# The gate products of a state-space branch, made in the linear-attention stage and kept in DRAM until the output stage

## The chip, the core and the metric

The kernel runs on one core of a Trainium2 chip. A core has five engines with instruction streams of their own: TensorE (PE, matrix products into PSUM), VectorE (DVE), ScalarE (ACT), GpSimd (POOL) and SyncE (SP), which here only starts transfers. The metric is the device time in microseconds; lower is better.

## The reference, cut to what matters

Two equal layers run one after the other over 2048 latent tokens and 128 context tokens. Each layer normalises `x` to `h`, projects `h` once, hands slices of the projection to three branches, and projects their joined outputs back:

```python
h = rms_norm(x, norm_w) * (1 + scale) + shift
z, xbc, dt, gq, gk, gv, gg, glr, aq, ak, av, ag = split_proj(h @ w_in)
y_ssd, _ = ssd_branch(z, xbc, dt, ...)       # state-space scan, both directions
y_gla, _ = gla_branch(gq, gk, gv, gg, glr, ...)   # linear attention
y_att = latent_attention(...) * silu(ag)     # windowed attention
x = x + gate * (concatenate([y_ssd, y_gla, y_att]) @ w_out)

# the end of ssd_branch:
y = y_f + flip(y_b) + xs * d_skip
y = rms_norm(y * silu(z), norm_w)
```

`z` (512 wide) depends on `h` alone, and is used only at the very end of the state-space branch.

## The kernel before

The 2176 tokens are 17 tiles of 128: the context tile (CT) and tiles 0 to 15. `h` is kept transposed for the whole layer as two fp16 parts (high and low), so `prod` (L281) makes a product of 256 columns as 24 matmuls of 128x256. A weight block of 256 columns is 1 MB; nine slots hold such blocks, and `ring` gives the next free one. `load_w` starts the transfer and splits the block into two fp16 parts on ACT and DVE (L246 to L265).

A layer has four stages.

1. The linear-attention (GLA) stage, `gla_phase`, goes through groups of tiles, CT alone first, then pairs. The generator `gla_group` makes the projections of a group (the first on the tile `HT`, the last a narrow one of 48 columns) and then, in the next group's turn, its chunk sums. Layer 0 takes the pairs upwards and makes `h` there, tile by tile; layer 1 takes them downwards, while the output stage of layer 0 has already made its `h`.
2. The attention stage, whose first matmuls after the GLA stage are `att_project`'s.
3. The state-space (SSD) stage: a convolution written as products, and a scan per tile.
4. The output stage, `out_tile`, in the order CT, 15, ..., 0. For each tile it fetches the branch outputs (`ym`), makes the gate product `z` (two products, 48 matmuls, L281, into `pz`), its Tanh (L1188) and gate (L1189), adds the backward scan's part (`pof`, L1197, L1200, L1201, with the carried state, L1203 and L1204), scales and squares (L1209, L1214), writes the normalised row in two fp16 parts to `yh` (L1231, L1232), has a DMA transpose it to `yt` (L1237), and makes four products with `w_out` (96 matmuls, into `po`), which L1247 and L1248 add to `x`. In layer 0 the same tile then makes the next layer's `h` (L429 to L466, another transpose). `yh` has one buffer, `yt` two.

The stages are written as Python generators that are stepped in turns; a scheduler then fixes the order of instructions on each engine at build time, so an engine works in that order and stops where its next instruction has to wait. All transfers are started by SP, in its order.

The two weight blocks of `z` (`wz0`, `wz1`) are loaded in the attention and SSD stages as loads 4 and 5 of `ssd_load`, and the four of `w_out` behind them; the last of those is converted on DVE (L264) while the scan is ending.

Of the kernel before, what the change touches and what calls it, by code (L numbers as in the profile page):

```python
# [10 lines left out]
F32 = mybir.dt.float32  # L11
# [9 lines left out]
P = 128  # L21
# [8 lines left out]
def host_constants(nt):  # L30
# [32 lines left out]
          ("sm", 512, 3), ("sxw", 512, 2), ("ssb", 512, 1), ("sy", 512, 2), ("sjd", 128, 1), ("scd", 8, 2)],  # L63
    "O": [("ym", 1024, 2), ("ct", 256, 2), ("sz1", 512, 1), ("oyo", 256, 1), ("sz0", 512, 1), ("yh", 1024, 1), ("yt", 1024, 2), ("xs", 1024, 2), ("gate", 1024, 1), ("otm", 512, 2),
          ("osb", 512, 1), ("hl", 1024, 1)],
# [3 lines left out]
START = {"A": 0, "T": 0, "C": 9600, "S": 0, "Q": 11136, "O": 0}  # L69
WORDS = 12768  # L70

# [7 lines left out]
def hybrid_kernel(ctx, tc, a, o):  # L79
# [146 lines left out]

    ring = [0, 1, 5, 7, 8, 2, 3, 6, 4]

# [76 lines left out]
    grow = [drp.tile([2, DM], F32, name=f"grow_{l}") for l in range(L)]  # L305
    mrow = [drp.tile([2, 2 * DM], F32, name=f"mrow_{l}") for l in range(L)]
    sct = [drp.tile([P, 2, P], F32, name=f"sct_{t}") for t in range(NTT)]
    sstb = [drp.tile([P, 512], F32, name=f"sstb_{t}") for t in range(NTT)]
# [166 lines left out]
    def gla_load(l, s, i):  # L475
        if i == 0:
            s.wqk, s.iqk = load_in(l, (1552, 1808), name="wqk")
        elif i == 1:
            s.wv, s.iv = load_in(l, (1808, 2064), name="wv")
        elif i == 2:  # L480
            s.wdl, s.idl = load_in(l, (1536, 1552), (2320, 2352), name="wdl", dst=k_wdl)

            s.aux = slot()
        else:
            s.wg, s.ig = load_in(l, (2064, 2320), name="wgg")

    def gla_begin(l, s, order):
# [502 lines left out]
    def ssd_load(l, s, i):  # L990

        if i < 4:
            w = load_in(l, (512 + 256 * i, 768 + 256 * i), name=f"wx{i}")
        elif i < 6:
            w = load_in(l, (256 * (i - 4), 256 * (i - 4) + 256), name=f"wz{i - 4}")
        else:
            w = load_w(a["w_out"], l, [(256 * (i - 6), 256 * (i - 6) + 256)], f"wo{i - 6}", row_scale=vec[l][:, 56:62])
        s.w.append(w)
# [157 lines left out]
    def out_begin(l, s):  # L1156
        s.wz, s.izh = [], []
        for j in range(2):
            w, iz = s.w[4 + j]
            izh = sb(f"izh{j}", [P, 1])  # L1160
            V.tensor_scalar(izh, iz, 0.5, None, ALU.mult)
            s.wz.append(w)
            s.izh.append(izh)
        s.wo, s.io = zip(*s.w[6:10])

        s.rows = halves(slot())
# [10 lines left out]
    def out_tile(l, s, t):  # L1177
# [89 lines left out]

    def gla_phase(l, s, order, before=None, after=None):

        prev, s.first = None, order[0]  # L1270
        for n, g in enumerate(order):
# [5 lines left out]
            run(prev)  # L1277
            step(cur)
            if after:
                after(n)  # L1280
            prev = cur
        run(prev)

    def loads(l, gla, att, ssd):

        todo = [(gla_load, gla, 0), (gla_load, gla, 1), (gla_load, gla, 2), (att_load, att, 0), (att_load, att, 1), (att_load, att, 2), (gla_load, gla, 3)]
        todo += [(ssd_load, ssd, i) for i in range(10)]

# [45 lines left out]
    def layer_state():  # L1334
        x = Gla(), Att(), Ssd()
        x[2].w = []
        return x
# [9 lines left out]

    gla_phase(0, gla, order0, enter, lambda n: load[0](3 + max(0, min(n - 3, 4))))
    for l in range(L):
        gla, att, ssd = state[l]  # L1350
        load[l](7)
        gla_states(l, gla)
        att_begin(l, att)
        load[l](8)
        gla_out_begin(l, gla)
# [15 lines left out]
        for t in range(NT):  # L1371
# [21 lines left out]
        for n, g in enumerate(order):  # L1393
# [8 lines left out]
            run(nxt)  # L1402
            load[l](13 + min(n, 3))
        load[l](17)
# [5 lines left out]
        for n in range(NTT):  # L1410
# [6 lines left out]
            run(tiles[n])  # L1417
            if l + 1 < L and n in (5, 8, 11):
                load[l + 1]((5, 8, 11).index(n) + 1)
        if l + 1 < L:  # L1420
            back = list(range(NG - 2, -1, -1))
            load[l + 1](3)
            gla_begin(l + 1, state[l + 1][0], back)
            gla_phase(l + 1, state[l + 1][0], [NG - 1] + back, None, lambda n: load[l + 1](3 + max(0, min(n, 4))))


def build(shapes, consts):
    import concourse.bacc as bacc

    nc = bacc.Bacc("TRN2", target_bir_lowering=False, num_devices=1, dynamic_dma_scratch_size=4096)  # L1430
    f32 = mybir.dt.from_np(np.dtype("float32"))
# [28 lines left out]
```

## Time and profile before

| what | us |
|---|---|
| median of 3 runs | 2339.43 (2337.83 to 2343.84) |
| the profiled execution: its own time | 2334.53 |
| the span that its trace covers | 2332.8 |
| TensorE busy in it | 2089.6 (90%) |
| VectorE, ScalarE, GpSimd busy | 1628.6, 991.8, 872.7 |

The profiled execution is 4.9 us below the median and 1.7 us above its own span. A share of busy time is a mean over stages that are limited by different things, so each stage is read by itself. In a row of the trace, "pd<-slot,HT" names the output and the operands by the program's names, and "[idle before <-releaser]" says how long the engine stood still before the row and what ended that.

### The profile page before, as it was taken

To read this page: it belongs to the slowest core of one execution; us is meant where nothing else is said; L and a number is where in the kernel's file an instruction comes from. 1 tells how busy PE (TensorE), PEld (TensorE's weight loads), DVE (VectorE), ACT (ScalarE), POOL (GpSimd) and SP (SyncE) were. 2 spreads that over 40 slices of the span, in tenths; PEclk is the share of its full clock that TensorE was granted. 3 is DMA by queue.
4 is the path that set the end of the run, shared out by engine and by line. 5 is a ranking of instruction groups with operands and counts; after the bars stand their busy time and mean duration, and the time that the engine had idled before them with its cause. 6 is when DMAs were issued, how large, how long until landed. Compare 5 with 4: busy or idle time off the path is not lost. (4 is left out here: it accounts for less than half of the span.)

```text
span 2332.8 us, 53735 instructions
## 1 busy us (share of the span) xinstructions
PE 2089.6 (90%) x21245; PEld 1735.9 (74%) x21245; DVE 1628.6 (70%) x4088; ACT 991.8 (43%) x2183; POOL 872.7 (37%) x906
## 2 busy tenths in 40 slices
PE   3688958899899999899999995888999999999998
PEld 0455747778787788788888884777878778878887
DVE  2566767887789888865564656777788988864442
ACT  2443545555445334433333643555563533422221
POOL 0010014566443444544431001456643344454442
PEclk6798979999999999999999997999999999999999
DMA  8697433567611013577656123456671101265643
GB/s 294 182 256 188 108 85 87 119 150 166 135 56 37 33 42 124 164 188 177 170 151 174 42 75 93 93 110 149 154 153 55 37 32 42 78 171 167 163 141 98
DMA packets 486353, 288.02 MB, mean 123 GB/s; under 512 B 354344, under 2 KB 447924, under 8 KB 483796
## 3 DMA queue, kind: packets, MB, share of 16 engines
q1 hardware_dynamic: 483796, 271.99, 44.5%
q0 software_dynamic: 2304, 12.58, 1.6%
q8 instruction: 167, 2.74, 0.5%
q14 instruction: 86, 0.70, 0.1%
HBM read 141.11 MB, written 64.93 MB: 88 GB/s over the span
## 5 line engine op out<-in xcount | busy, mean ns | idle before, releaser
L281 PEld LDWEIGHTS <-HT 128*128 128x128 f16 x6528 | 585.3, 100 | 170.8 <-issue 93.0
L281 PE MATMUL pd<-slot,HT 128*128 128x256 f16 x3456 | 432.1, 278 | 50.0 <-ACT work L806 29.7
L281 PEld LDWEIGHTS <-slot 128*128 128x128 f16 x4320 | 394.3, 97 | 105.9 <-issue 41.2
L281 PE MATMUL pd<-slot,work 128*128 128x256 f16 x3264 | 365.5, 273 | 2.1 <-DMA work<-work 2.1
L281 PEld LDWEIGHTS <-work 128*128 128x128 f16 x3264 | 319.2, 98 | 42.6 <-DMA work<-work 2.6
L281 PE MATMUL pd<-HT,slot 128*128 128x260 f16 (+3 forms) x2592 | 316.5, 269 | 13.2 <-DMA HT<-work 12.4
L281 PE MATMUL ps<-HT,slot 128*128 128x260 f16 (+1 forms) x1728 | 201.5, 270 | 4.5 <-DVE work L1054 4.5
L281 PE MATMUL ps<-slot,HT 128*128 128x256 f16 x1440 | 175.6, 281 | 19.1 <-ACT work L1188 14.3
L1248 POOL TENSOR_TENSOR work<-work 128x512 f32<-128x512 f32 x68 | 89.2, 1312 | 185.5 <-DVE work L1247 176.3
L875 POOL TENSOR_TENSOR work<-work 128x512 f16<-128x512 f32 (+2 forms) x102 | 117.4, 1154 | 85.1 <-ACT work L874 70.3
L1054 DVE SCALAR_TENSOR_TENSOR work<-ps,work 128x256 f32<-128x256 f32 (+1 forms) x288 | 134.0, 465 | 11.9 <-ACT work L1052 7.6
L1054 DVE SCALAR_TENSOR_TENSOR work<-pd,work 128x256 f32<-128x256 f32 (+1 forms) x288 | 132.5, 464 | 3.7 <-ACT work L1052 0.9
L872 ACT ACTIVATE work<-ps,nm,K 128x512 f32<-128x512 f32 (+2 forms) x136 | 100.9, 744 | 73.1 <-DVE nm L864 58.3
L1116 POOL TENSOR_TENSOR work<-work 128x512 f32<-128x512 f32 x68 | 73.2, 1081 | 113.3 <-ACT work L1074 61.8
L1056 ACT ACTIVATE work<-work 128x256 f32<-128x256 f32 (+1 forms) x144 | 58.1, 403 | 121.0 <-DVE work L1054 82.8
L1088 POOL TENSOR_TENSOR work<-K,work 128x512 bf16<-128x512 bf16 x68 | 72.2, 1063 | 77.9 <-PE ps L1100 77.2
L281 PE MATMUL pm<-slot,HT 128*128 128x256 f16 x816 | 98.8, 277 | 1.6 <-DVE work L907 1.5
L854 PEld LDWEIGHTS <-work 128*128 128x128 f16 x1008 | 74.4, 98 | 34.7 <-issue 31.9
L874 ACT CAST work<-work 128x512 f16<-128x512 f32 (+2 forms) x136 | 78.1, 589 | 46.2 <-DMA slot<-work 26.3
L669 POOL MEMSET work<- 128x512 f32 x2 | 1.1, 525 | 256.2 <-PE pm L616 256.2
L1057 DVE SCALAR_TENSOR_TENSOR work<-work 128x256 f32<-128x256 f32 (+1 forms) x144 | 81.9, 569 | 19.1 <-ACT work L1056 18.0
L1214 ACT ACTIVATE work<-work 128x512 bf16<-128x512 f32 x68 | 42.7, 629 | 119.2 <-DMA work<-work 53.6
(374 smaller groups left out, 4035.1 us busy)
## 6 DMA issues: line engine op xcount, KB each, us to landing
slot<-in_w_in_dram SPq DMA_DIRECT2D x24, 1024.0 KB
ymix<-work SPq DMA_DIRECT2D x68, 128.0 KB
yacc<-work SPq DMA_DIRECT2D x34, 256.0 KB
work<-ymix SPq DMA_DIRECT2D x34, 256.0 KB
work<-yacc SPq DMA_DIRECT2D x34, 256.0 KB
x<-work SPq DMA_DIRECT2D x17, 512.0 KB
work<-x SPq DMA_DIRECT2D x17, 512.0 KB
out_dram<-work SPq DMA_DIRECT2D x17, 512.0 KB
```

The lines of the kernel that those rows point to most:

```text
L281: T.matmul(out, lhsT=lhs(i, k), rhs=rhs(j, k), start=(n == 0), stop=(n == 3 * KB - 1))
L854: T.matmul(ps[:, bs], lhsT=s.qt[t][:, 2 * gg + kv], rhs=kt[:, 2 * kv + j], start=(j == 0), stop=(j == 1 and mk is None))
L872: S.activation(pr, sc[hh][:, :nb * P], AF.Exp, scale=s.isc[:, 0:1], bias=nm[:, hh:hh + 1], accum_out=ls[:, hh:hh + 1])
L874: S.copy(p16[:, 0], pr)
L875: (G if hh else V).tensor_tensor(p16[:, 1], pr, p16[:, 0], ALU.subtract)
L1054: V.scalar_tensor_tensor(acc[:, jj, :W], pp[:, q:q + W], s.cw[j][:, q, jj:jj + 1], acc[:, jj, :W], ALU.mult, ALU.add)
L1056: S.activation(th[:, :W], acc[:, jj, :W], AF.Tanh)
L1057: V.scalar_tensor_tensor(acc[:, jj, :W], th[:, :W], 1.0, acc[:, jj, :W], ALU.add, ALU.mult)
L1088: G.tensor_tensor(sr[:, j:j + 4], oh[:, j:j + 4].unsqueeze(2).to_broadcast([P, 4, P]), at.unsqueeze(1).to_broadcast([P, 4, P]), ALU.mult)
L1116: G.tensor_tensor(xw, x, bc8(s.wst[:, t, 8 * d:8 * d + 8]), ALU.mult)
L1214: S.activation(junk, ym[:, 512 * i:512 * i + 512], AF.Square, accum_out=ss[:, i:i + 1])
L1248: G.tensor_tensor(xs[:, js], xs[:, js], tm, ALU.add)
```

## The change

The gate products leave `out_tile`. A new `gate_tile` makes them in `gla_phase`: after each group's first step, for the tiles of the group before, and for the last group after its last step. It copies each half from PSUM to SBUF on ACT and stores it in DRAM (`zraw`). `out_tile` loads the tile's 512 columns back and takes the Tanh from there. The loads of the two weight blocks move to the GLA stage of the same layer (layer 0) or to the end of layer 0's output stage (layer 1), and the blocks of `w_out` come correspondingly earlier. The number of matmuls is the same. Per layer there are 34 more copies on ACT, 34 more stores (128 KB each) and 17 more loads (256 KB each).

```diff
-    ring = [0, 1, 5, 7, 8, 2, 3, 6, 4]
+    ring = [0, 1, 5, 7, 8, 2, 3, 4, 6]
...
+    def gate_load(l, s, i):
+        w, iz = load_in(l, (256 * i, 256 * i + 256), name=f"wz{i}")
...
+    def gate_tile(s, t):
+
+        pz = psum(None, "d")
+        for j in range(2):
+            js = slice(256 * j, 256 * j + 256)
+            prod(pz[:, js], hs(t), lambda q, k: s.wz[j][:, q, k, :])
+            z = k_hx[1][:, js]
+            S.copy(z, pz[:, js])
+            D.dma_start(zraw[t][:, js], z)
...
-        pz = psum(None, "d" if t in (CT, NT - 1) else "s")
-        sz = sb(rot(("sz0", "sz1"), "sz"), [P, 512])
+        z = sb("zl", [P, 512])
+        D.dma_start(z, zraw[t])
+        sz = sb("sz", [P, 512])
         for j in range(2):
             js = slice(256 * j, 256 * j + 256)
-            prod(pz[:, js], hs(t), lambda q, k: s.wz[j][:, q, k, :])
-            S.activation(sz[:, js], pz[:, js], AF.Tanh, scale=s.izh[j])
-        V.scalar_tensor_tensor(sz, sz, 1.0, pz, ALU.add, ALU.mult)
+            S.activation(sz[:, js], z[:, js], AF.Tanh, scale=s.izh[j])
+        V.scalar_tensor_tensor(sz, sz, 1.0, z, ALU.add, ALU.mult)
...
             run(prev)
             step(cur)
+            if n:
+                for t in GROUPS[order[n - 1]]:
+                    gate_tile(gates, t)
             if after:
                 after(n)
             prev = cur
         run(prev)
+        for t in GROUPS[order[-1]]:
+            gate_tile(gates, t)
...
-            for at, n in ((1, 9), (4, 10), (7, 11), (13, 12), (15, 13)):
+            for at, n in ((4, 11), (6, 12), (8, 13), (13, 14), (15, 15)):
```

Not shown: the order list of `loads` (the two gate blocks stand behind the third GLA block), the pool table (`zl` with two buffers in place of a second `sz`, the pool 768 words longer) and a smaller DMA scratch.

TensorE at the end of layer 0's GLA stage. Before, the last narrow projection (48 wide) is followed by the attention's two products (`slot7`, `slot8`), and between them stand the chunk sums of the last two groups (L589, L596):

```order
L281 MATMUL pd_3365<-K_77,HT_83 128x48
...
L281 MATMUL pd_3722<-slot7_74,HT_83 128x256
...
L281 MATMUL pd_3722<-slot8_75,HT_83 128x256
...
L281 MATMUL pd_3792<-slot7_74,HT_83 128x256
...
L281 MATMUL pd_3792<-slot8_75,HT_83 128x256
...
L589 MATMUL ps_3443<-work_66 64x64 x4
```

In the changed program the `z` products of four tiles (`pd_4171`, `pd_4224`, `pd_4433`, `pd_4486`; `slot7` and `slot8` now hold `wz0` and `wz1`) stand there, and the attention's (`pd_4688`, from `slot2`) follow. L607 is the old L589:

```order
L281 MATMUL pd_4171<-slot7_74,HT_83 128x256
...
L281 MATMUL pd_4224<-slot7_74,HT_83 128x256
...
L281 MATMUL pd_4433<-slot7_74,HT_83 128x256
...
L281 MATMUL pd_4433<-slot8_75,HT_83 128x256
...
L281 MATMUL pd_4486<-slot8_75,HT_83 128x256
...
L607 MATMUL ps_4303<-work_66 64x64 x4
...
L281 MATMUL pd_4688<-slot2_69,HT_83 128x256
```

So 192 matmuls of the gate stand ahead of the attention's 96, and all but three of them ahead of the last group's sums; in layer 1 it is the same.

VectorE in layer 0's output stage, where it writes the second fp16 part of a tile's row (L1232 before, L1241 after; `zc_13594` and `osc_13599` belong to one tile) and evicts a half of `po` (L1247, L1256; `osc` tells the tile). Before:

```order
L1247 SCALAR_TENSOR_TENSOR work_66<-pd_13478,osc_13171,work_66 128x512
L1216 TENSOR_SCALAR zss_13585<-zss_13585 128x1
...
L1224 TENSOR_TENSOR zc_13594<-zrs_13590,zc_13594 128x1
L1232 SCALAR_TENSOR_TENSOR work_66<-work_66,zc_13594 128x512 x2
L1247 SCALAR_TENSOR_TENSOR work_66<-pd_13529,osc_13171,work_66 128x512
L1228 TENSOR_SCALAR osc_13599<-zrb_13597 128x1
```

After, where `zc_14032` and `osc_14037` belong to one tile and `osc_13882` to the tile before it:

```order
L1233 TENSOR_TENSOR zc_14032<-zrs_14028,zc_14032 128x1
L1237 TENSOR_SCALAR osc_14037<-zrb_14035 128x1
L1241 SCALAR_TENSOR_TENSOR work_66<-work_66,zc_14032 128x512
L1256 SCALAR_TENSOR_TENSOR work_66<-pd_14071,osc_13882,work_66 128x512
L462 SCALAR_TENSOR_TENSOR work_66<-work_66,rs_14047,slot0_67 128x1024
L1241 SCALAR_TENSOR_TENSOR work_66<-work_66,zc_14032 128x512
```

Before, a tile's row was finished behind the eviction of the first half of the product two tiles ahead of it (between `osc_13171` and `osc_13599` lies one more tile, `osc_13396`). After, in 8 of the 15 pairs of neighbours in layer 0, the row is finished only behind the eviction of the first half of the very next tile's product; in the other pairs, and in layer 1, the distance is two, as before.

SP near the start of layer 0 (L350, L351 fetch `w_ada`; L466, L467 transpose `h`). Before:

```order
L350 DMA slot3_70<-in_w_ada_dram 128x1024 x2
L466 DMA_TRANSPOSE HT_83<-work_66 128x16x128
L1304 DMA slot5_72<-in_x_sample_dram 128x1024
L466 DMA_TRANSPOSE HT_83<-work_66 128x16x128
```

After:

```order
L467 DMA_TRANSPOSE HT_83<-work_66 128x16x128
L1318 DMA slot6_73<-in_x_sample_dram 128x1024
L467 DMA_TRANSPOSE HT_83<-work_66 128x16x128
L1318 DMA slot5_72<-in_x_sample_dram 128x1024
L619 DMA sqin_16_168<-work_66 32x2x128 x3
L351 DMA slot2_69<-in_w_ada_dram 128x1024
```

The four `w_ada` transfers of that place now stand behind the transposes of the first tiles.

## Rows read from the trace of the kernel before

**Rows 1.** The page: the span in 40 slices of 58.3 us, TensorE's busy tenths.
```profile
PE   3688958899899999899999995888999999999998
```

**Rows 2.** Windows: length, busy us (count) by engine, granted clock, DMA share, GB/s.
```profile
80.00:280.00 200.00, 161.09 (x2341) 118.59 (x2338) 126.02 (x308) 90.16 (x184) 16.69 (x29) 0.91 0.69 182
80.00:120.00 40.00, 26.38 (x298) 18.93 (x295) 22.75 (x47) 16.61 (x38) 4.63 (x8) 0.83 0.65 166
1280.00:1400.00 120.00, 119.66 (x2152) 100.63 (x2151) 76.09 (x238) 63.36 (x133) 0.00 (x0) 1.00 0.20 58
1000.00:1200.00 200.00, 190.33 (x1653) 167.03 (x1651) 120.09 (x243) 67.73 (x133) 92.42 (x92) 0.97 0.65 172
```

**Rows 3.** Timeline of TensorE, early layer 0: start, us, line, idle before.
```profile
93.53 4.43 PE L281 MATMUL pd<-HT,slot 128*128 128x256 f16 x25 [11.17 <-DMA HT<-work]
```

**Rows 4.** Timeline of TensorE, end of the GLA stage in layer 0, then layer 1.
```profile
282.90 2.23 PE L281 MATMUL pd<-slot,HT 128*128 128x256 f16 x19
...
301.99 0.54 PE L589 MATMUL ps<-work 32*64 32x64 f32 x32 [1.86 <-DVE work L578]
...
330.40 1.87 PE L281 MATMUL pd<-slot,HT 128*128 128x256 f16 x8 [15.34 <-ACT work L806]
...
1390.91 2.23 PE L281 MATMUL pd<-slot,HT 128*128 128x256 f16 x19
...
1409.49 0.54 PE L589 MATMUL ps<-work 32*64 32x64 f32 x32 [2.07 <-DVE work L578]
```

**Rows 5.** Timelines of SP and ACT, end of layer 1's GLA stage: a store and its waiter.
```profile
1397.06 6.07 SPq L599 DMA_DIRECT2D oacc<-work  x2
...
1402.41 0.37 ACT L598 COPY work<-pm 128x256 f32<-128x256 f32 x1 [4.99 <-DMA oacc<-work]
```

**Rows 6.** Timeline of TensorE, layer 0: last convolution product, `po` of tile 15, next layer.
```profile
922.15 2.86 PE L281 MATMUL ps<-HT,slot 128*128 128x260 f16 x24
...
987.99 10.64 PE L281 MATMUL pd<-slot,work 128*128 128x256 f16 x96
...
1249.38 2.84 PE L281 MATMUL pd<-HT,slot 128*128 128x128 f16 x48
```

**Rows 7.** Timeline of TensorE, layer 1, from the last convolution product to the end.
```profile
2024.82 2.86 PE L281 MATMUL ps<-HT,slot 128*128 128x260 f16 x24
...
2078.28 3.98 PE L281 MATMUL pd<-slot,work 128*128 128x256 f16 x35
...
2142.40 1.03 PE L1197 MATMUL ps<-K,work 128*128 128x256 f32 x4
2143.27 2.13 PE L281 MATMUL pd<-slot,work 128*128 128x256 f16 x18
2145.23 2.78 PE L281 MATMUL ps<-slot,HT 128*128 128x256 f16 x24
...
2299.75 27.02 PE L281 MATMUL pd<-slot,work 128*128 128x256 f16 x246
```

**Rows 8.** Timelines of SP and ACT, one tile of layer 1's output stage.
```profile
2156.56 1.91 SPq L1237 DMA_TRANSPOSE work<-work  x1
...
2160.62 0.63 ACT L1214 ACTIVATE work<-work 128x512 bf16<-128x512 f32 x1 [0.95 <-DMA work<-work]
...
2166.85 0.63 ACT L1214 ACTIVATE work<-work 128x512 bf16<-128x512 f32 x1 [1.73 <-DVE work L1209]
...
2173.15 1.83 SPq L1237 DMA_TRANSPOSE work<-work  x1
```

**Rows 9.** Timelines of SP, ACT, DVE, layer 0's output stage: transpose, landing, vector work.
```profile
1122.11 2.02 SPq L1237 DMA_TRANSPOSE work<-work  x1
...
1126.37 0.63 ACT L1214 ACTIVATE work<-work 128x512 bf16<-128x512 f32 x1 [1.06 <-DMA work<-work]
...
1129.53 1.22 DVE L462 TENSOR_TENSOR work<-work,slot 128x1024 f32<-128x1024 f32 x1
...
1137.03 0.75 DVE L1247 SCALAR_TENSOR_TENSOR work<-pd,osc,work 128x512 f32<-128x512 f32 x1
```

More of the change, by code (lines that the diff above doesn't have):

```diff
@@ L63 @@
           ("sm", 512, 3), ("sxw", 512, 2), ("ssb", 512, 1), ("sy", 512, 2), ("sjd", 128, 1), ("scd", 8, 2)],
-    "O": [("ym", 1024, 2), ("ct", 256, 2), ("sz1", 512, 1), ("oyo", 256, 1), ("sz0", 512, 1), ("yh", 1024, 1), ("yt", 1024, 2), ("xs", 1024, 2), ("gate", 1024, 1), ("otm", 512, 2),
+    "O": [("ym", 1024, 2), ("ct", 256, 2), ("zl", 512, 2), ("oyo", 256, 1), ("sz", 512, 1), ("yh", 1024, 1), ("yt", 1024, 2), ("xs", 1024, 2), ("gate", 1024, 1), ("otm", 512, 2),
           ("osb", 512, 1), ("hl", 1024, 1)],
@@ L69 @@
 START = {"A": 0, "T": 0, "C": 9600, "S": 0, "Q": 11136, "O": 0}
-WORDS = 12768
+WORDS = 13536
 ONCE = ("bm", "bn", "bx", "hcl", "hpb", "hrb", "hc", "hci")
@@ L306, in hybrid_kernel @@
     mrow = [drp.tile([2, 2 * DM], F32, name=f"mrow_{l}") for l in range(L)]
+    zraw = [drp.tile([P, 512], F32, name=f"zraw_{t}") for t in range(NTT)]
     sct = [drp.tile([P, 2, P], F32, name=f"sct_{t}") for t in range(NTT)]
@@ L485, in gla_load @@
             s.wg, s.ig = load_in(l, (2064, 2320), name="wgg")
+    def gate_load(l, s, i):
+        w, iz = load_in(l, (256 * i, 256 * i + 256), name=f"wz{i}")
+        izh = sb(f"izh{i}", [P, 1])
+        V.tensor_scalar(izh, iz, 0.5, None, ALU.mult)
+        s.wz.append(w)
+        s.izh.append(izh)
+    def gate_tile(s, t):
[6 more added lines that the diff above has]
+            D.dma_start(zraw[t][:, js], z)
     def gla_begin(l, s, order):
@@ L993, in ssd_load @@
             w = load_in(l, (512 + 256 * i, 768 + 256 * i), name=f"wx{i}")
-        elif i < 6:
-            w = load_in(l, (256 * (i - 4), 256 * (i - 4) + 256), name=f"wz{i - 4}")
         else:
-            w = load_w(a["w_out"], l, [(256 * (i - 6), 256 * (i - 6) + 256)], f"wo{i - 6}", row_scale=vec[l][:, 56:62])
+            w = load_w(a["w_out"], l, [(256 * (i - 4), 256 * (i - 4) + 256)], f"wo{i - 4}", row_scale=vec[l][:, 56:62])
         s.w.append(w)
@@ L1156, in out_begin @@
     def out_begin(l, s):
[L1157 to L1164, printed above, removed]
+        s.wo, s.io = zip(*s.w[4:8])
         s.rows = halves(slot())
@@ L1266, in step, with gla_phase @@
             next(x, None)
-    def gla_phase(l, s, order, before=None, after=None):
+    def gla_phase(l, s, gates, order, before=None, after=None):
         prev, s.first = None, order[0]
@@ L1282, in gla_phase @@
         run(prev)
+        for t in GROUPS[order[-1]]:
+            gate_tile(gates, t)
     def loads(l, gla, att, ssd):
-        todo = [(gla_load, gla, 0), (gla_load, gla, 1), (gla_load, gla, 2), (att_load, att, 0), (att_load, att, 1), (att_load, att, 2), (gla_load, gla, 3)]
-        todo += [(ssd_load, ssd, i) for i in range(10)]
+        todo = [(gla_load, gla, 0), (gla_load, gla, 1), (gla_load, gla, 2), (gate_load, ssd, 0), (gate_load, ssd, 1), (att_load, att, 0), (att_load, att, 1), (att_load, att, 2), (gla_load, gla, 3)]
+        todo += [(ssd_load, ssd, i) for i in range(8)]
         def upto(n):
@@ L1335, in layer_state @@
         x = Gla(), Att(), Ssd()
-        x[2].w = []
+        x[2].w, x[2].wz, x[2].izh = [], [], []
         return x
@@ L1346, in hybrid_kernel @@
     gla_begin(0, gla, order0[1:])
-    gla_phase(0, gla, order0, enter, lambda n: load[0](3 + max(0, min(n - 3, 4))))
+    gla_phase(0, gla, state[0][2], order0, enter, lambda n: load[0](5 + max(0, min(n - 3, 4))))
     for l in range(L):
         gla, att, ssd = state[l]
-        load[l](7)
+        load[l](9)
         gla_states(l, gla)
         att_begin(l, att)
-        load[l](8)
+        load[l](10)
         gla_out_begin(l, gla)
@@ L1402, in hybrid_kernel @@
             run(nxt)
-            load[l](13 + min(n, 3))
+            load[l](15 + min(n, 2))
         load[l](17)
@@ L1417, in hybrid_kernel @@
             run(tiles[n])
-            if l + 1 < L and n in (5, 8, 11):
-                load[l + 1]((5, 8, 11).index(n) + 1)
+            if l + 1 < L and n in (5, 8, 11, 13):
+                load[l + 1]((5, 8, 11, 13).index(n) + 1)
         if l + 1 < L:
             back = list(range(NG - 2, -1, -1))
-            load[l + 1](3)
+            load[l + 1](5)
             gla_begin(l + 1, state[l + 1][0], back)
-            gla_phase(l + 1, state[l + 1][0], [NG - 1] + back, None, lambda n: load[l + 1](3 + max(0, min(n, 4))))
+            gla_phase(l + 1, state[l + 1][0], state[l + 1][2], [NG - 1] + back, None, lambda n: load[l + 1](5 + max(0, min(n, 4))))
 def build(shapes, consts):
     import concourse.bacc as bacc
-    nc = bacc.Bacc("TRN2", target_bir_lowering=False, num_devices=1, dynamic_dma_scratch_size=4096)
+    nc = bacc.Bacc("TRN2", target_bir_lowering=False, num_devices=1, dynamic_dma_scratch_size=1024)
     f32 = mybir.dt.from_np(np.dtype("float32"))
```

## The prediction, made before the changed kernel had run

> **What bounds the kernel now.** I read the page's slices first, then windows of the stages that the change touches, then the timelines of each engine at their seams.
>
> The slices [rows 1] say that TensorE is full for most of the span: of 40 slices 26 show a 9, and the thin ones are the start, the seams and the early layer 0. So a product that moves from one full stage to another changes nothing; what counts is whether a stage has room, and whether the stage it leaves has another limit close below. Windows tell the stages apart [rows 2]. Layer 0's GLA stage has TensorE busy 161.1 of 200 us from 80 to 280, with 38.9 idle; the granted clock is 0.91 on average and 0.83 in the first 40 us. Layer 1's GLA stage has it busy 119.7 of 120 us at clock 1.00: no room at all. Layer 0's output stage is at 190.3 of 200 with transfers at a share of 0.65; layer 1's runs with TensorE full.
>
> The unit of every sum: 18 matmuls of 128x256 start to start take 1.96 us [rows 7], so one takes 0.109. One tile's gate is 48 of them, 5.24 us; its `po` is 96, 10.5 us, and `pof` adds 0.87 (2142.40 to 2143.27). All 17 gates of a layer are 89 us.
>
> **The change part by part.**
>
> *Layer 0's GLA stage, 13 tiles inside the groups.* 13 x 5.24 = +68. Of the 38.9 idle us, 11.2 are one wait for the first tiles' transpose [rows 3], and the transposes now stand ahead of four `w_ada` transfers on SP, so I take 6 off it (bounds 0 and 11). Of the other 27.7 the gate fills some: it has its operands early and stands where TensorE waits for the chunk sums. I take 18 (bounds 0 and 27.7). At clock 0.83 a share of the stretch ran at the lower of the two levels (1.2 and 2.4 GHz); the engine had been idle for a third of it. With more work that share should fall; 6 off (bounds 0 and 7, since 0.17 x 40 us is 7). Sum **+38**, bounds +22 and +68.
>
> *The seam to the attention, both layers.* The last four tiles' gates (192 matmuls, 20.9 us) now stand between the last GLA projection and the attention's products. Before, TensorE began the last group's sums 19.1 us after that projection (282.90 to 301.99), and its third attention product came at 330.40 after 15.3 us of idling, behind a chain through those sums and ScalarE's L806 [rows 4]. After, 189 gate matmuls (20.6) and the older group's sums (6.7 us: 19.1 less the 10.5 of the attention's 96 matmuls and less the 1.86 of the wait) stand ahead of the last group's sums: 27.3, 8 later. The attention's 96 now mix with those sums, 10.5 us where TensorE had some idle time; I add 2. So **+10** in layer 0, and in layer 1 (18.6 us between the same points [rows 4]) **+10**. Bounds each: 0 (VectorE sets the chain and the gate is all hidden) and 21 (none is).
>
> *Layer 1's GLA stage, 13 tiles.* No idle time to fill: +68, less 2 for small gaps; **+66**, bounds 62 and 72.
>
> *ScalarE and the stores.* 34 copies of 128x256 per layer on an engine that is busy 63.4 of 120 us in layer 1's stage [rows 2]; by the 0.37 us of the copy L598 of that size [rows 5] they take 13 us beside TensorE. Their stores join SP's queue. Nothing is added for them: a copy must have landed before the same half is written for the next tile, at least 5.24 us later, and the nearest row is a copy that ran 5.35 us after the first of two stores was begun (1397.06 to 1402.41) [rows 5]. That is about even, so its bounds are 0 and some stall (rival 3).
>
> *The output stages.* In layer 0, 65.8 us pass from the last convolution product to `po` of tile 15, and 261.4 from there to the next layer's first product: (261.4 - 10.6) / 15 = 16.7 us per tile [rows 6]. In layer 1 it is 53.5, and 248.5 to the end: (2326.77 - 2078.28 - 10.6) / 15 = 15.9 [rows 7]. Gates of four to five tiles lie ahead of tile 15, the rest in the pace.
> Without the gate TensorE needs 11.35 us per tile. The next limit is the one buffer `yh`: transpose, its landing, Square, scaling, `yh`, next transpose. In layer 1 the transpose takes 4.06 us to land (2156.56 to 2160.62), the first Square 0.8, and from the second Square to the next transpose 6.30 (2166.85 to 2173.15) [rows 8]: 11.2, so TensorE and this loop are even. I take 11.8 for what they cost each other: 15 x (15.9 - 11.8) = **-61** (bounds 11.35 and 13: -68 and -44).
> In layer 0, by the new order of VectorE, 8 of 15 tiles finish `yh` only behind the eviction of the first half of the product just ahead. That loop is 5.24 (half of `po`) + 0.75 (eviction) + 1.22 (L462 between) + 0.75 (the second part) + 0.5 to SP + 4.26 for the transpose [rows 9], 12.7, and more when a transpose lands late beside the transfers of this stage. I take 13.5 for these and 12.4 for the rest, 13.0 on average: 15 x (16.7 - 13.0) = **-55** (bounds 11.35 and 15.5: -80 and -18).
> Ahead of tile 15 the gate gave TensorE work between scan steps and was partly hidden there; the conversion of the last `w_out` block also leaves VectorE. I take **-14** in layer 0 and **-8** in layer 1 (bounds 0 and the gates' own 21 to 26). Together 69 of the 89 us come back in each layer, the rest is lost to the loops.
> The reload of `zraw` is 256 KB per tile, issued tiles ahead; it is hidden unless it delays the transposes behind it on SP, which is in the bound of 15.5.
>
> **The sum.** +38 +10 +66 +10 -14 -55 -8 -61 = -14. Against the profiled execution's own 2334.5 (span 2332.8 and 1.7 outside) that is 2320.5; this execution is 4.9 below the median of the runs shown, so **2325** on the median's scale.
>
> **The rivals.** 0.3%, 7 us, is about what a measurement of this kernel can tell from no change.
>
> 1. *Slower: layer 0's output stage keeps its pace.* It is the stage where the loop behind `yh` is longest, where transfers already have a share of 0.65 [rows 2] and where the gate's reload joins them. At 15.5 us per tile it gives back 18 instead of 55: +23, about 2362. It decides from 14.4 per tile on (-14 + 15 x 1.4 = +7). Against it: the parts of that loop measured above end at 12.7.
>
> 2. *No difference: the work is moved, not hidden.* If layer 0's GLA stage fills only half of what I take (9 of 18) and the clock gives nothing (6), the sum is +1: 2340, and 2332 to 2346 counts as the same. That stage's TensorE waits on chains and transfers that the gate doesn't shorten, with transfers at 0.69 [rows 2], which speaks for it; against it, the gate's operands are there early.
>
> 3. *Slower: the single buffer between gate and store.* Where a store takes 8 us instead of 5.35, ScalarE waits some 2.8 us before the second tile of each pair and holds everything behind it, 8 pairs in two layers: +44 if TensorE feels it all, +25 if a little over half, 2350. The Trainium skill (Trainium Kernel Development and Optimization, Best Practices) asks for double buffers so that transfers overlap computing; by that rule this single buffer costs something, and no row of before shows it yet. The Trainium skill (DMA: Bandwidth & Descriptors, Anatomy of one DMA) puts a transfer's fixed cost at about 2 us, most of it the confirmation of the write; by that figure alone the wait would be nothing. From the rows, 5.35 us against 5.24 between writes, it is about even.
>
> 4. *Faster than I say:* TensorE sets both output stages (11.35 per tile: -25 and -7 more) and the GLA stage of layer 0 fills all (-16): about 2277 at the most, 2295 with a part of it.
>
> **How the numbers follow.** My case, within 15 us of 2325, has 0.44; rival 1 0.16, rival 2 0.18, rival 3 0.08, rival 4 0.14. Most of my case, 0.42, lies below the 7 us, and rival 4 is all there: faster 0.56. The same: rival 2 and what is left of mine, 0.20. Slower: rivals 1 and 3, 0.24. The range leaves out the far half of rivals 1 and 4: 2294 to 2355; the likeliest case's own is 2310 to 2340.
>
> **What will show it.** In the trace after: gate products in the GLA stages with TensorE's idle time there down by about 20 us in layer 0; the first product of layer 1's GLA stage some 20 us earlier than 1249 (+48 - 69) and, after +76 there, layer 1's last stage beginning some 55 us later; output tiles 13 and 11.8 us apart; the wait at the seam (L806's successor) 10 us later than the last GLA projection plus 47.5. I am wrong if output tiles in layer 0 stay above 14.4 us, if ScalarE waits for the stores of `zraw` by more than 1 us each, or if the seams take more than 60 us.

## The result, and the profile after

The changed kernel takes 2439.34 us (median of 4 runs, 2420.14 to 2449.94) against 2341.64 (4 runs): the ratio is 1.0398, with an interval of 1.0344 to 1.0451. Beside the last experiments it was run once more: 2436.97 us, ratio 1.0384 (1.0350 to 1.0417). It was forecast at 2325; it is 98 us slower than the kernel before.

The profiled execution took 2439.11 us, with a span of 2437.2, so 104.4 more than the span of before. Its timeline of TensorE at the seams of the stages, in order of time:

```profile
85.23 6.99 PE L281 MATMUL pd<-HT,slot 128*128 128x256 f16 x48 [1.72 <-DMA HT<-work]
164.31 6.73 PE L281 MATMUL pd<-slot,HT 128*128 128x256 f16 x48 [17.12 <-DVE work L553]
187.37 4.29 PE L281 MATMUL pd<-slot,HT 128*128 128x256 f16 x22 [6.08 <-ACT K L502]
365.14 0.74 PE L281 MATMUL pd<-K,HT 128*128 128x48 f16 x23
424.24 5.28 PE L281 MATMUL pd<-slot,HT 128*128 128x256 f16 x24 [16.24 <-ACT work L824]
1029.22 2.86 PE L281 MATMUL ps<-HT,slot 128*128 128x260 f16 x24
1094.59 5.63 PE L281 MATMUL pd<-slot,work 128*128 128x256 f16 x50 [0.35 <-DMA work<-work]
1314.79 2.84 PE L281 MATMUL pd<-HT,slot 128*128 128x128 f16 x48
1523.33 0.74 PE L281 MATMUL pd<-K,HT 128*128 128x48 f16 x23
1583.68 4.37 PE L281 MATMUL pd<-slot,HT 128*128 128x256 f16 x24 [14.07 <-ACT work L824]
2190.83 2.86 PE L281 MATMUL ps<-HT,slot 128*128 128x260 f16 x24
2419.78 11.30 PE L281 MATMUL pd<-slot,work 128*128 128x256 f16 x102
```

Three rows of the kernel before belong beside them: the last narrow projection of layer 0, the same in layer 1, and layer 1's third attention product (L824 is the old L806):

```profile
282.29 0.76 PE L281 MATMUL pd<-K,HT 128*128 128x48 f16 x24
1390.30 0.77 PE L281 MATMUL pd<-K,HT 128*128 128x48 f16 x24
1436.74 4.64 PE L281 MATMUL pd<-slot,HT 128*128 128x256 f16 x21 [14.38 <-ACT work L806]
```

The distances between the rows after, set beside the same distances between these and in [rows 4], [rows 6] and [rows 7], divide the 104 us up to 0.2. A GLA stage ends where its last narrow projection does, so 282.29 + 0.76 = 283.05 before and 365.14 + 0.74 = 365.88 after:

| stretch | before | after | change | forecast |
|---|---|---|---|---|
| layer 0: start to last GLA projection | 283.1 | 365.9 | +82.8 | +38 |
| seam to the third attention product | 47.3 | 58.4 | +11.0 | +10 |
| attention and SSD, to the last convolution product | 591.8 | 605.0 | +13.2 | 0 |
| from there to `po` of tile 15 | 65.8 | 65.4 | -0.5 | -14 |
| `po` of tile 15 to layer 1's first product | 261.4 | 220.2 | -41.2 | -55 |
| layer 1: GLA stage | 141.7 | 209.3 | +67.6 | +66 |
| seam | 45.7 | 59.6 | +13.9 | +10 |
| attention and SSD | 588.1 | 607.2 | +19.1 | 0 |
| from there to the end | 302.0 | 240.3 | -61.7 | -69 |

Windows of the profile after, with the columns of [rows 2] (length; busy us of TensorE, its weight loads, VectorE, ScalarE, GpSimd; clock; DMA share; GB/s):

```profile
80.00:280.00 200.00, 157.24 (x1855) 112.46 (x1858) 106.53 (x240) 77.31 (x151) 16.20 (x29) 0.88 0.80 192
280.00:365.00 85.00, 84.87 (x1251) 72.69 (x1248) 40.96 (x122) 36.57 (x74) 0.00 (x0) 1.00 0.16 50
1320.00:1520.00 200.00, 199.75 (x2904) 171.46 (x2909) 90.51 (x258) 84.04 (x181) 0.28 (x1) 1.00 0.22 62
1094.60:1314.80 220.20, 187.13 (x1577) 160.48 (x1578) 176.20 (x314) 87.12 (x165) 124.83 (x113) 0.95 0.83 222
```

From 80 to 280 us TensorE is busy for 157.2 us, where it was busy for 161.1 [rows 2]: the gate did not go into the idle time, it took the place of the groups' work, and that work now lies behind 280, in 85 us of a full TensorE. Layer 1's GLA stage is full as before, only longer.

How a gate product comes to stand still, the 17.12 us before 164.31 in the timeline above, is seen in rows of SyncE, ScalarE and VectorE ahead of it:

```profile
138.32 7.96 SPq L467 DMA_TRANSPOSE HT<-work  x1
...
161.65 1.04 ACT L464 CAST work<-slot 128x1024 f16<-128x1024 f32 x1 [20.05 <-DMA HT<-work]
...
164.01 0.24 DVE L553 TENSOR_SCALAR work<-pd,wdli 128x32 f32<-128x32 f32 x1
```

A transpose of `h`, begun at 138.32, is waited for until 161.65 by ScalarE's L464, which needs its source buffer for the next tile. VectorE stands behind L464, and so does its L553, which empties the GLA projection out of one of the two PSUM buffers "d". The next product on TensorE, the gate of the second tile of a pair, needs that buffer, and the next group's projections stand behind it in TensorE's order. So the gate can't use the wait, and holds up what comes after. In the second profile of the same program this wait is 6.8 us long, so its size is that of one execution. Over the stage, waits of L281's products for L553 and L502, which empty these two buffers, come to 27.2 us in the first profile and 17.8 in the second; in the kernel before no product of L281 in this stage waits for L535, the old L553.

### The profile page after: what moved, and what is told of

It reads as the page before. It is cut to its first block, busy times and chain, and to the rows that moved or that the text cites. A ratio compares the mean times of both kernels' runs of the same rounds, so it can differ in the third digit from the quotient of the medians.

```text
span 2437.2 us, 54024 instructions
## 1 busy us (share of the span) xinstructions
PE 2129.9 (87%) x21245; PEld 1755.6 (72%) x21245; DVE 1660.5 (68%) x4088; ACT 1011.5 (42%) x2249; POOL 903.5 (37%) x906
## 5 line engine op out<-in xcount | busy, mean ns | idle before, releaser
L281 PEld LDWEIGHTS <-HT 128*128 128x128 f16 x6528 | 586.0, 100 | 172.0 <-issue 70.0
L281 PE MATMUL pd<-slot,HT 128*128 128x256 f16 x4896 | 608.5, 281 | 67.5 <-ACT work L824 30.3
L281 PEld LDWEIGHTS <-slot 128*128 128x128 f16 x4320 | 397.3, 98 | 112.5 <-issue 46.9
L281 PE MATMUL pd<-slot,work 128*128 128x256 f16 x3264 | 374.2, 278 | 40.9 <-DMA work<-work 34.0
L281 PEld LDWEIGHTS <-work 128*128 128x128 f16 x3264 | 324.3, 100 | 91.9 <-DMA work<-work 39.3
L281 PE MATMUL pd<-HT,slot 128*128 128x260 f16 (+3 forms) x2592 | 317.7, 272 | 11.4 <-ACT K L502 4.0
L281 PE MATMUL ps<-HT,slot 128*128 128x260 f16 (+1 forms) x1728 | 202.3, 271 | 5.0 <-DVE work L1070 5.0
L1257 POOL TENSOR_TENSOR work<-work 128x512 f32<-128x512 f32 x68 | 100.5, 1479 | 148.1 <-DVE work L1256 119.4
L893 POOL TENSOR_TENSOR work<-work 128x512 f16<-128x512 f32 (+2 forms) x102 | 123.0, 1209 | 87.4 <-ACT work L892 67.5
L1132 POOL TENSOR_TENSOR work<-work 128x512 f32<-128x512 f32 x68 | 72.5, 1069 | 103.8 <-ACT work L1090 54.0
L892 ACT CAST work<-work 128x512 f16<-128x512 f32 (+2 forms) x136 | 77.7, 586 | 50.1 <-DMA slot<-work 26.3
L281 PE MATMUL pm<-slot,HT 128*128 128x256 f16 x816 | 97.2, 276 | 1.5 <-DVE wpb L193 1.2
L872 PE MATMUL ps<-work 128*128 128x128 f16 x752 | 78.4, 222 | 22.7 <-DMA work<-work 22.7
L1073 DVE SCALAR_TENSOR_TENSOR work<-work 128x256 f32<-128x256 f32 (+1 forms) x144 | 81.7, 568 | 19.1 <-ACT work L1072 18.4
L875 DVE TENSOR_REDUCE mx<-ps 128x1 f32<-128x512 f32 (+2 forms) x136 | 82.5, 642 | 13.6 <-PE ps L874 11.1
```

The costliest lines, as they stand in the source:

```text
L281: T.matmul(out, lhsT=lhs(i, k), rhs=rhs(j, k), start=(n == 0), stop=(n == 3 * KB - 1))
L872: T.matmul(ps[:, bs], lhsT=s.qt[t][:, 2 * gg + kv], rhs=kt[:, 2 * kv + j], start=(j == 0), stop=(j == 1 and mk is None))
L875: V.tensor_reduce(mx[:, hh:hh + 1], ps[:, :nb * P], AX.X, ALU.max)
L892: S.copy(p16[:, 0], pr)
L893: (G if hh else V).tensor_tensor(p16[:, 1], pr, p16[:, 0], ALU.subtract)
L1073: V.scalar_tensor_tensor(acc[:, jj, :W], th[:, :W], 1.0, acc[:, jj, :W], ALU.add, ALU.mult)
```

## The experiments

Layer 0's GLA stage ("stage" below) is given from its first product to its last narrow projection. Before, in the changed kernel, and in its second profile:

```profile
71.48:283.05 211.57, 172.32 (x2494) 127.79 (x2493) 133.18 (x323) 96.84 (x195) 17.24 (x30) 0.91 0.70 186
69.58:365.88 296.30, 251.97 (x3220) 193.80 (x3220) 154.09 (x377) 120.39 (x234) 16.75 (x30) 0.91 0.60 148
69.35:360.75 291.40, 255.94 (x3220) 195.00 (x3220) 153.84 (x377) 120.00 (x234) 16.75 (x30) 0.91 0.58 151
```

Each run has one profile. Three of the runs below (the late `w_out` blocks, two buffers for `yh`, no reload) have the changed kernel's order of TensorE, ScalarE and SP in this stage, and took 288.2, 296.7 and 287.5 us: the same program spreads over 287.5 to 296.7, so a difference of less than some 9 us shows nothing here. With the seam, to the third attention product, the five take 345.4 to 355.5 us.

**The gate left out (a floor for everything else).**

```diff
-            if n:
-                for t in GROUPS[order[n - 1]]:
-                    gate_tile(gates, t)
...
-        for t in GROUPS[order[-1]]:
-            gate_tile(gates, t)
...
-        D.dma_start(z, zraw[t])
+        D.dma_start(z, yacc[t])
```

> The changed kernel with the gate products and their stores left out; the output stage loads yacc where it loaded zraw, so the gate's values are wrong and everything else is done. It shows what the removal is worth by itself. Theory A (all 17 gates of a layer are paid in full where they now stand, about 83 + 11 us in layer 0 and 68 + 14 in layer 1, and the output stages give back 42 and 62): about 2437 - 176 = 2260 (2250 to 2275), with the GLA stages as long as in the kernel before. Rival B (the new loads and buffers slow the stages by themselves): layer 0's GLA stage is still longer than before by 15 us or more, and the attention and SSD stages stay 13 and 19 us longer in either case if the moved loads of w_out are their cause: then their length is the changed kernel's, not the one before.

Measured: 2271.09 us, ratio 0.9692 (0.9663 to 0.9721), so taking the gate out of the output stages, with all else that the change does, is worth some 74 us, and putting it where it now stands costs 166. Timeline of TensorE of this run, at the same seams:

```profile
283.62 0.38 PE L281 MATMUL pd<-K,HT 128*128 128x48 f16 x9
332.71 5.28 PE L281 MATMUL pd<-slot,HT 128*128 128x256 f16 x24 [15.33 <-ACT work L824]
933.96 2.86 PE L281 MATMUL ps<-HT,slot 128*128 128x260 f16 x24
997.91 2.32 PE L281 MATMUL pd<-slot,work 128*128 128x256 f16 x10 [3.79 <-DMA work<-work]
1226.07 2.84 PE L281 MATMUL pd<-HT,slot 128*128 128x128 f16 x48
1368.40 0.77 PE L281 MATMUL pd<-K,HT 128*128 128x48 f16 x24
1417.73 2.51 PE L281 MATMUL pd<-slot,HT 128*128 128x256 f16 x11 [14.70 <-ACT work L824]
```

Layer 0's GLA stage takes 214.5 us. The earlier transpose does shorten its wait, from 11.2 us [rows 3] to 1.8, and the stage's idle time falls from 39.3 to 30.4 us. But TensorE is busy for 184.1 us in place of 172.3, with 18 more matmuls (16 of them of `w_ada`, some 4 us) and at a granted clock of 0.89 in place of 0.91, so the stage without a gate is not shorter than before. In the three runs below that put the gates behind the last group, the same stage took 217.9 to 224.0 us, where the kernel before took 211.6 and, with the small scratch, 206.0: what else the change does there, the two moved block loads among it, comes to 3 to 18 us more. The gate's price, GLA stage and seam together, is 354.7 - 263.2 = 91.4 us in layer 0 and 268.9 - 191.7 = 77.2 in layer 1, against 89 us of its matmuls; measured from the longer stages of those three runs it would be 3 to 10 us less in layer 0. From the last convolution product to `po` of tile 15 it takes 64.0 us with no gate in it at all, nearly as before with the gate (65.8 [rows 6]; 4.9 tiles' gate products stand there by the count of matmuls): they cost almost nothing between the scan steps. In the attention and SSD stages this run took 601.2 and 601.8 us, 23 more than before with nothing of the gate in them; so by stages the removal is worth 88 us in this profile, and 64 remain.

**The gate at the end of the stage.**

```diff
-            if n:
-                for t in GROUPS[order[n - 1]]:
-                    gate_tile(gates, t)
...
-        for t in GROUPS[order[-1]]:
-            gate_tile(gates, t)
+        for g in order:
+            for t in GROUPS[g]:
+                gate_tile(gates, t)
```

> The changed kernel with all gate products of a layer behind its last linear-attention group, where nothing can be filled but the seam. Theory A (inside the groups the gate fills nothing): the last narrow projection stands near 283 again and the third attention product near 283 + 89 + 15 = 387 to 405, against 424 in the changed kernel; layer 1 gains some 15 at its seam too; in all 2375 to 2415. Rival (inside the groups it does fill idle time, and something else makes the stage long): the third attention product at 424 or later, in all 2435 or more.

Measured: 2402.79 us, ratio 1.0265 (1.0206 to 1.0324). Timeline of TensorE:

```profile
292.52 0.77 PE L281 MATMUL pd<-K,HT 128*128 128x48 f16 x24
419.64 0.60 PE L281 MATMUL pd<-slot,HT 128*128 128x256 f16 x4 [2.24 <-ACT work L824]
```

The time was as expected, the stage was not: the third attention product stands at 419.6, not at 387 to 405. Stage and seam cost 86.1 and 79.8 us over the run without a gate, nearly what they cost inside the groups. So nearly all of the gate's 89 us is paid in either place; of the seam's idle time only some 11 us are used (126.4 - 48.7 = 77.7 us in layer 0). What this run gained lies for the most part in its attention and SSD stages (594.5 and 584.1 us, 33.5 of the 37.6 us between the two profiles).

**No stores; stores started by ScalarE.**

```diff
-            D.dma_start(zraw[t][:, js], z)
+            S.dma_start(zraw[t][:, js], z)
```

The first of the two runs leaves this line out and loads `yacc` in place of `zraw`.

> The changed kernel with the gate products and their copies, but without the stores to zraw; the output stage loads yacc in its place, so the gate's values are wrong. Theory A (the gate waits behind ScalarE's and the projections' waits and fills nothing): layer 0's GLA stage ends within 10 us of the changed kernel's 366, in all 2415 to 2437. Rival B (the stores crowd the transfers between 120 and 200 us and hold the single buffer): that stage ends 25 us or more earlier, about 2400 or less.

> The changed kernel with the stores to zraw started by ScalarE in place of SyncE. Theory Q (on SyncE the store's trigger waits for the copy, 45 us in all in layer 0, and the next tiles' loads and transposes of h stand behind it): layer 0's GLA stage takes about 282 us in place of 296, as without the stores. Rival B (the stores' bytes crowd the other transfers): it stays at 290 or more.

Measured: without stores 2425.23 us, ratio 1.0340 (1.0300 to 1.0380), stage 281.7; from ScalarE 2394.49, ratio 1.0209 (1.0172 to 1.0246), stage 289.0. Without stores the stage is 6 to 15 us shorter than the changed kernel's five, which is neither expectation's number, and layer 1's stage and seam are no shorter (272.9 us, against 268.9 and 267.9). With the stores on ScalarE the stage lies inside the spread, so no price of SyncE's trigger is shown. The second run's lower time is for the most part not from this stage: its attention and SSD stages took 591.1 and 590.7 us.

**The copy on VectorE; the product in the other PSUM buffers.**

```diff
-            S.copy(z, pz[:, js])
+            V.tensor_copy(z, pz[:, js])
```

and, by itself,

```diff
-        pz = psum(None, "d")
+        pz = psum(None, "s")
```

> The changed kernel with the gate's halves copied out of PSUM by VectorE in place of ScalarE. Theory A2 (inside the groups the gate fills nothing because its copies stand in ScalarE's order behind waits for transposes, up to 20 us): layer 0's GLA stage takes 275 us or less in place of 296, in all 2415 or less. Rival A3 (the order on TensorE itself and the chains of the groups leave nothing to fill, whoever copies): 285 to 305 us, in all within 15 us of 2439.

> The changed kernel with the gate's product in the other pair of PSUM buffers, which the chunk sums use and the projections don't. Theory A1 (the gate waits for the two buffers that it shares with the projections, as in the 17.1 us wait at 164): layer 0's GLA stage takes 275 us or less in place of 296, in all 2415 or less. Rival A3 (nothing to fill): 285 to 305 us, within 15 us of 2439; it may also get longer where the chunk sums now wait for these buffers.

Measured: VectorE 2419.15 us, ratio 1.0320 (1.0292 to 1.0348), stage 288.1; other buffers 2421.43, ratio 1.0321 (1.0292 to 1.0350), stage 272.7. The copy on VectorE leaves the stage inside the spread, so ScalarE's order is not what holds the gate; that run's total lies below its range for this case, and its attention and SSD stages took 594.4 and 603.3 us. With the product in the buffers "s", of which there are four and not a pair, the stage is 15 to 24 us shorter, as Theory A1 had it, but the total is not at 2415 or less, and a part comes back at the seam, where the third attention product now stands 63.9 us behind the last narrow projection in place of 58.4:

```profile
405.99 4.18 PE L281 MATMUL pd<-slot,HT 128*128 128x256 f16 x22 [14.69 <-ACT work L824]
```

Stage and seam take 336.6 us, 9 to 19 less than the changed kernel's; in layer 1, where the stage has hardly any idle time, they take 272.1 against 268.9 and 267.9. So the shared buffers are a part of the price, 9 to 19 us of 91. The window of the stage with the other buffers, and of the stage without a gate:

```profile
69.30:342.10 272.80, 245.30 (x3136) 189.67 (x3136) 150.00 (x366) 118.20 (x232) 17.45 (x30) 0.94 0.58 159
```

```profile
69.50:284.00 214.50, 184.11 (x2512) 135.20 (x2512) 142.61 (x352) 105.46 (x204) 18.90 (x30) 0.89 0.70 195
```

Even with buffers of its own the gate leaves 27.5 us idle where the stage without it leaves 30.4. Its 624 matmuls here add 61.2 us of TensorE's time and not 68, at a clock of 0.94 in place of 0.89. So the higher clock can give back at most some 7, and the idle time 3. What keeps the gate out of the rest of the idle time when the buffers are apart was not found.

**Both at once.**

> The gate's product in the other pair of PSUM buffers and its stores started by ScalarE. If the shared buffers and the trigger that waits on SyncE each cost what they cost alone (24 and 7 of the 296 us of layer 0's GLA stage), it takes 260 to 272; the floor without any gate is 214.5, so at least 45 of the 68 us of its gate products are still paid. Rival (the same wait seen twice): 270 to 285. In all 2375 to 2420, above the kernel before in either case.

Measured: 2431.60 us, ratio 1.0381 (1.0352 to 1.0410), stage 274.4. That is the rival's range: with the buffers apart, the store's engine gives nothing more. By the spread it may have given nothing before either, and then there was no second wait to see. The total lies above the expected 2375 to 2420; the attention and SSD stages took 603.0 and 610.0 us.

**The small scratch, and the w_out blocks.**

```diff
-((4, 11), (6, 12), (8, 13), (13, 14), (15, 15))
+((4, 11), (6, 12), (8, 13))
...
-            load[l](15 + min(n, 2))
+            load[l](13 + min(n, 4))
```

is the second run; the first is the kernel before with the scratch of 1024.

> The kernel before with the small DMA scratch alone. Theory A: no change, 2335 to 2348. Rival C (the small scratch slows GpSimd's own transfers of w_ada, seen as 14.5 us to landing in place of 7.7): layer 0's GLA stage ends 10 us or more later than 283, so 2350 to 2370.

> The changed kernel with the four w_out blocks loaded one after another during the scans, none in the attention stage. If the moved loads are why attention and SSD stages together took 605 and 607 us in place of 592 and 588: they come back to 595 and 592 or less, in all about 2410. Rival (the order that the scheduler found and its stalls, not the loads): they stay above 600 in both layers, in all 2430 to 2450, or more, since the last block is then converted at the end of the scan again.

Measured: 2345.52 us, ratio 1.0011 (0.9982 to 1.0039), and 2426.98 us, ratio 1.0350 (1.0298 to 1.0402), with 606.7 and 601.6 us in the attention and SSD stages. Neither the scratch nor the time of those loads is a cause. (The kept trace of the changed kernel has a median of 9.0 us to landing for the transfers of `w_ada` that the first expectation puts at 14.5.)

**Two buffers for yh; no reload.** The pool's `yh` gets a second buffer, `zl` and `ct` lose one; in the other run `z = yf` stands for the load.

> The changed kernel with two buffers for yh (and one instead of two for zl and ct, to make room). Theory: without the gate the loop through the one yh buffer and the transpose sets the pace of layer 0's output tiles, 14.0 us, and adds a little to layer 1's 11.8: layer 0's output stage from po of tile 15 takes 185 to 205 in place of 220, layer 1's 180 to 184 in place of 186; in all about 20 to 30 less than the changed kernel. Rival (transfers at a share of 0.6 to 0.9 set layer 0's pace, whatever the buffers): 215 to 225.

> The changed kernel with the gate made and stored as there, but not loaded back: the output stage takes the Tanh and the product from its own tile of the scan's result, so the gate's values are wrong. Theory T (transfers set layer 0's output tiles, at a share of 0.83 and 222 GB/s; 256 KB of some 3.1 MB per tile are gone): layer 0 from po of tile 15 takes 200 to 210 in place of 220, layer 1 stays at 184 to 187. Rival D (VectorE's order and the transpose loop, not the bytes): 215 to 225.

Measured: 2406.32 us, ratio 1.0249 (1.0204 to 1.0295), layer 0 from `po` of tile 15 to the next layer 214.1 us and layer 1 180.4 to the end; and 2416.54 us, ratio 1.0299 (1.0251 to 1.0346), layer 0 221.3 and layer 1 190.0. One tile of the changed kernel, from SyncE, TensorE and VectorE, shows the loop:

```profile
1194.92 2.01 SPq L1246 DMA_TRANSPOSE work<-work  x1
...
1199.39 10.64 PE L281 MATMUL pd<-slot,work 128*128 128x256 f16 x96
...
1206.36 0.74 DVE L1256 SCALAR_TENSOR_TENSOR work<-pd,osc,work 128x512 f32<-128x512 f32 x1
1207.02 1.28 DVE L462 SCALAR_TENSOR_TENSOR work<-work,rs,slot 128x1024 f32<-128x1024 f32 x1
1208.21 0.75 DVE L1241 SCALAR_TENSOR_TENSOR work<-work,zc 128x512 f16<-128x512 f32 x1
...
1208.99 1.58 SPq L1246 DMA_TRANSPOSE work<-work  x1
```

It is the loop that was forecast, 14.07 us long instead of 12.7 to 13.5: the product begins 4.5 us after the transpose and its first half is evicted 7.0 us later. But a second buffer takes only 6 us of 220 away, and 256 KB less per tile none. So neither the buffer alone nor the bytes hold layer 0's pace. VectorE is busy for 176 of the 220 us, and `zl` and `ct` lost a buffer in that run, which may hide a part of its gain; which limit lies behind the loop was not found. In layer 1 the second buffer gave 5 to 6 us, as expected: (180.4 - 10.6) / 15 = 11.3 us per tile, what the prediction has for TensorE alone. The rest of the first run's lower total is mostly layer 1's attention and SSD stages, 590.3 us in place of 607.1.

**What gained, put together.** Gates at the end with stores from ScalarE, and the same with two `yh`:

> The gates behind the last group, and their stores started by ScalarE. If what each gained adds up (28 by the place, 20 to 35 by the store's engine, of which part lies inside the groups and is gone here): 2375 to 2395. Still above the kernel before, since the gate's price in the linear-attention stage stays about 80 us a layer and the output stages give back 40 to 61.

> As the one with the gates at the end and stores from ScalarE, with two buffers for yh as well. The best version that these experiments point to with the gate moved: 2350 to 2375 if the yh loop was layer 0's limit; 2375 to 2395 if it was the transfers. It beats the kernel before (2345) only if layer 0's output stage falls to about 180.

Measured: 2410.05 us, ratio 1.0264 (1.0225 to 1.0302), and 2410.40, ratio 1.0281 (1.0213 to 1.0348). Both are above what was expected: the gains do not add up, and no version with the gate moved comes near the kernel before. The second buffer for `yh` gave 2 us in layer 0 here (222.4 in place of 224.8) and 5 in layer 1 (179.9 in place of 185.1). The run of the changed kernel beside them:

> The changed kernel once more, unaltered, beside the other runs of this chip, since its four earlier times lie between 2420 and 2450. Expected 2420 to 2450 again. If it is at 2420, the variants that came to 2419 to 2427 (the copy on VectorE, the other PSUM buffers, the late w_out blocks, no store) gained nothing in total; at 2440 they gained 15.

Measured: 2436.97 us, ratio 1.0384 (1.0350 to 1.0417). Beside it the copy on VectorE (1.0320) and the other buffers (1.0321) are faster by some 15 us, with intervals that end where this one begins; for no store (1.0340) and the late `w_out` blocks (1.0350) the intervals overlap.

**What the runs say together of the attention and SSD stages.** The work there is the same in every run with the gate moved, but the order of TensorE's instructions that the scheduler found is not, even where the edit lies in the output stage alone. In layer 1, eight profiles whose order differs from the changed kernel's at fewer than 450 of 5081 places took 599.9 to 610.0 us; five that differ at 1179 places or more took 584.1 to 590.7. Between them lies the run with the late `w_out` blocks (1047 places, 601.6). The changed kernel, and two buffers for `yh`, which differ at 2219 places:

```profile
1583.68:2190.83 607.15, 555.57 (x5081) 460.11 (x5081) 487.21 (x1209) 283.60 (x675) 287.31 (x293) 0.97 0.34 84
```

```profile
1574.31:2164.57 590.26, 551.13 (x5082) 457.02 (x5081) 483.70 (x1210) 281.89 (x675) 283.37 (x293) 0.98 0.35 86
```

In layer 0 the changed kernel's order, to within 96 places, took 598.9 to 609.5 us in five profiles and other orders took 591.1 to 606.7, so there the two overlap. The order goes with the time; no run sets it by itself, and which stall it makes was not looked for.

## Why the prediction was wrong

*The step that failed* is "Of the other 27.7 the gate fills some: it has its operands early and stands where TensorE waits for the chunk sums. I take 18 (bounds 0 and 27.7)." In its place the runs showed a gate that is paid in full: stage and seam of layer 0 take 91 us more than without it and 94 more than before, where 48 were forecast. The idle time did not go into the gate: the stage leaves 44.3 and 35.5 us idle in the changed kernel's two profiles, 39.3 before, and 30.4 to 40.9 in the four runs with no gate product inside the groups. Having its operands early was no help, since TensorE works in order and the gate's next buffer is one that a projection still holds. That is shown for a part: buffers of its own cost 9 to 19 us less, no stores 5 to 15 less (stage and seam). What holds the rest stays open. The same step took 6 us for the earlier transpose and 6 for the clock. The transpose came earlier and the idle time fell with it, but TensorE's busy time rose by more; and a higher clock is seen only in some runs (0.94 with the other buffers; 0.91 before and in the changed kernel). This is 45 of the 118 us by which the sum was off.

*Ahead of tile 15*, -14 and -8 were taken off and nothing came: the gates had cost next to nothing there. That is the other half of why moving them loses: of 89 us per layer the old place hid 21 to 26. Layer 0's stretch, before and after, shows what took their place:

```profile
922.15:987.99 65.84, 58.47 (x458) 48.99 (x457) 52.03 (x123) 27.34 (x52) 34.97 (x32) 0.95 0.56 166
```

```profile
1029.22:1094.59 65.37, 45.96 (x232) 34.44 (x231) 46.32 (x107) 23.83 (x42) 35.45 (x30) 0.71 0.59 179
```

TensorE stands idle for 19.4 us in place of 7.4, 13.1 of them in waits for the carried state (L1213, the old L1204; 25.4 us in both layers, 1.2 before). And with the gate's 235 matmuls gone, the granted clock is 0.71 in place of 0.95, a mean of stretches at the two levels, so the 232 matmuls that are left take 46.0 us; in layer 1 it is 0.75 in place of 1.00. How much the scan's chain by itself and how much the lower clock kept these stretches at 65 and 54 us was not tested.

*The output stages.* Layer 1's pace was right (11.7 us, forecast 11.8), and by the run with two `yh` the loop named was its cause. Layer 0's came to 14.0 instead of 13.0, inside its bounds, 14 us of the sum. There the loop is in the rows, but a second buffer gave 2 to 6 us where 15 to 35 were expected of it, so that the number lay within its bounds is partly luck.

*Layer 1's GLA stage and the seams* were right: +67.6 for +66, +11.0 and +13.9 for +10 each.

*The attention and SSD stages*, 13 and 19 us longer, were put at nothing, without a reason. In the runs these two stages took between 584 and 610 us per layer, in the kernel before 588 to 594. The time of the moved loads is excluded; the order that the scheduler found goes with it, and that it is the cause is likely but not shown.

*The rivals.* The second, "the work is moved, not hidden", named the mechanism, but let half of the 18 us be filled. The third, the single buffer, is in the trace four times: ScalarE's L502 waits 15.9 us for a store in all, three of the four behind 365 us, at the seams; it is too small to decide. Here the Trainium skill's advice to double-buffer (Trainium Kernel Development and Optimization, Best Practices) points at a real wait, and these waits are a small part of the loss. The first rival did not come about.

## What to carry to other kernels

Idle time of an engine in a stage is not room for other work unless that work can go on while the stage's own instructions wait: ask which buffers it shares with them and what stands in front of it in its engine's order. Before moving work out of a full stage, leave it out altogether for one run: that run gives what the removal is worth (74 us here) and what the new place costs (166). Work that lies between the steps of a dependent chain can already be free, as here, and a sum by busy time then overrates its removal. And where a scheduler fixes the order anew for every version, compare stages before totals, and the same program with itself first: two versions can differ by 17 us in a stage that neither of them edits.

## What the runs showed that was not expected

A DMA transpose of one tile of `h`, begun at 138.32 us and waited for until 161.65, in a stage where the DMA share is 0.8, took some 23 us; in layer 1's quieter output stage one of the same size landed in 4.06 [rows 8]. Not all transfers are started by SP: 16 of `w_ada` in layer 0's GLA stage are started by GpSimd, and the three begun beside that transpose, from 141.5 to 148.2, took 16.4 to 20.0 us to land, the other 13 between 4.6 and 12.6. Which of them held up which is not shown.

And a change whose products lie in the GLA and output stages moved the attention and SSD stages by up to 19 us per layer, and its variants by up to 22, with TensorE's busy time there 549 to 559 us for the same matmuls. The granted clock went with it: 0.98 before, 0.96 in the longest.
